# Seven instead of five Strassen pairs in the second feed-forward product, with two sums of weight blocks added by DMA

## The chip, the core and the metric

The kernel runs on one core of a Trainium2 chip. The metric is the device time of one execution in microseconds, the median over runs. A profile is one execution with every instruction, semaphore event and DMA recorded. TensorE is called PE here, VectorE DVE, ScalarE ACT, GpSimd POOL, SyncE SP.

## The reference

One layer of a decoder trunk over 256 positions of width 1024: RMS norm, attention with 8 heads of 128 (one block of 256, causal), residual add, RMS norm, a SwiGLU mixer with 2816 hidden columns, residual add, final RMS norm. All in float32. What the change touches is the last product of the SwiGLU:

```python
def swiglu(h, w_in, w_out):
    g, u = jnp.split(jnp.einsum('bsd,df->bsf', h, w_in), 2, axis=-1)
    return jnp.einsum('bsf,fd->bsd', jax.nn.silu(g) * u, w_out)
```

Here `silu(g) * u` is 256 x 2816 and `w_out` is 2816 x 1024.

## The kernel before

Every float32 product is made of three matmuls of a faster kind (`mm`, L93): an operand is split into a high half (a cast on ACT) and a low half (a subtraction on DVE), and high x high, high x low and low x high are added in PSUM. So every weight tile of 128 x 2048 that a DMA brings (`raw`) has to be turned into `hi` and `lo` before PE can use it. The pool `wpool` has four buffers of each of these three; `weights()` takes the next one of each, and a buffer comes free when its last reader has finished.

The second product adds up over NC = 11 row-tile pairs of `w_out` (256 rows each, laid out as 128 x 2048). A plain pair takes `eight_mm`: 8 products of 128 x 128 by 128 x 512, 24 matmuls. A pair whose number is in SEVEN (L49) takes `seven_mm` (L426): Strassen's scheme for the 2 x 2 blocks, 7 products, 21 matmuls. It needs four sums of blocks of the hidden activations, made once in `turn` (L361), and four sums of weight blocks, made in `load_out` (L390): the first two by one add of 1024 columns on DVE (L404), then one each of 512 columns (L410, L412). A Strassen pair therefore takes two buffers of `raw`, `hi` and `lo`: the first for the plain blocks, of which 1536 columns are split, the second (`rs`, `hs`, `ls`) for the four sums.

The order of the pairs is 0 to 8 (`TAIL` = 9), then pairs 9 and 10, which are always plain and are split over the output corners at the end, so that the final norm can begin early. The seven PSUM accumulators of Strassen's scheme live through all pairs; the plain pairs add into four of them (`corners`), and after pair 8 the corner sums are put together on DVE (L457 to L466). `turn` of a pair runs on PE, ACT and DVE beside the first product (`hidden`), one pair behind it. Which instruction of DVE, ACT and SP stands before which is fixed when the program is built; each engine works its list in order, and an instruction that waits holds up all behind it. All loads of weights go through SP's queue; POOL has nothing to do after the start.

`held` (L65) lets big tiles that are used one after another share memory; `HAT` gives the columns that a pair takes in them, 896 for a Strassen pair, 512 for a plain one.

Of the kernel before, what the change touches and what calls it, by code (L numbers as in the profile page):

```python
# [26 lines left out]
F32 = mybir.dt.float32  # L27
F32R = mybir.dt.float32r
AF = mybir.ActivationFunctionType
ALU = mybir.AluOpType  # L30
AX = mybir.AxisListType

P = 128
T = 256
# [3 lines left out]
H = 8  # L38
# [7 lines left out]
XK = 4  # L46


SEVEN = (0, 2, 4, 6, 8)  # L49
HALF = 5  # L50
HAT = [sum(896 if d in SEVEN else 512 for d in range(c)) for c in range(NC + 1)]


@with_exitstack
def trunk(ctx, tc, xT, x, g2, g3, wv, wqk, wo, w_in, w_out, out):
    nc = tc.nc
# [8 lines left out]
    def held(n, dtype, slot):  # L65
        return home.tile([P, SLOTS[slot]], dtype, name=slot)[:, :n]
# [7 lines left out]
    def weights():  # L74
        return [wpool.tile([P, 2048], d, name=n) for d, n in ((F32, "raw"), (F32R, "hi"), (F32R, "lo"))]
# [12 lines left out]
    def load(src, pieces=2):  # L88
        tiles = weights()
        fetch(tiles, src, 0, 2048, pieces)  # L90
        return tiles[1:]

    def mm(o, lh, ll, rh, rl, first, last):  # L93
        nc.tensor.matmul(o, lhsT=lh, rhs=rh, start=first, stop=False)  # L94
        nc.tensor.matmul(o, lhsT=lh, rhs=rl, start=False, stop=False)  # L95
        nc.tensor.matmul(o, lhsT=ll, rhs=rh, start=False, stop=last)  # L96
# [39 lines left out]
    with tc.tile_pool(name="attn2", bufs=2) as a2:  # L136
        xh = const.tile([P, KD, T], F32R, name="xh")
        xl = const.tile([P, KD, T], F32R, name="xl")
        oh, ol = held(2 * H * T, F32R, "first").rearrange("p (i h t) -> i p h t", i=2, h=H)

        third = held(D + T + 18 * P, F32, "third")
        v1, rbc = third[:, :D], third[:, D : D + T]
# [4 lines left out]
        for k in range(KD):  # L147
# [13 lines left out]
            else:  # L161
                a = k % 2 * 1024
# [40 lines left out]
        def project(h):  # L203
            wh, wl = (w.rearrange("p (k n) -> p k n", k=KD) for w in wk.pop(h))
            pk = ps_a.tile([P, 2, T], F32, name="pa") if h < 2 else ps_mm.tile([P, 2, T], F32, name="pmm")
            for j in range(2):
                js = slice(j * P, (j + 1) * P)
                for k in range(KD):
                    mm(pk[:, j], wh[:, k, js], wl[:, k, js], xh[:, k], xl[:, k], k == 0, k == KD - 1)

            f = a2.tile([P, 2 * T], F32, name="qk")
            nc.vector.tensor_tensor(
                f.rearrange("p (j t) -> p j t", j=2), pk, rbc[:, None, :].to_broadcast([P, 2, T]), op=ALU.mult
            )
            fh = a2.tile([P, 3 * P], F32R, name="qkh")
            fl = a2.tile([P, 3 * P], F32R, name="qkl")
            nc.scalar.copy(fh, f[:, P:])
            nc.vector.tensor_sub(fl, f[:, P:], fh.bitcast(F32))
            qk[h] = f, fh, fl
# [22 lines left out]
        def transpose_p(h):  # L242
            pp = ps_a.tile([P, 3 * P], F32, name="pa")
            for i in range(3):
                nc.tensor.transpose(pp[:, i * P : (i + 1) * P], pn[h][:, i * P : (i + 1) * P], ident)  # L245
            p0h = a2.tile([P, T], F32R, name="p0h")
            p0l = a2.tile([P, T], F32R, name="p0l")
            p1 = a2.tile([P, P], F32, name="p1")
            nc.scalar.copy(p0h, pp[:, :T])
            nc.vector.tensor_sub(p0l, pp[:, :T], p0h.bitcast(F32))  # L250
            nc.scalar.copy(p1, pp[:, T:])
            pt[h] = p0h, p0l, p1
# [11 lines left out]
        def follow(h):  # L264

            for step, i in ((attend, h - 3), (scores, h - 1), (transpose_p, h - 2)):
                if 0 <= i < H:
                    step(i)

        for h in range(H):  # L270
            if h > 1:
                wk[h] = load(wqk[h])
            project(h)
            follow(h)
# [48 lines left out]
    with tc.tile_pool(name="ffn2", bufs=2) as f2:  # L323
# [3 lines left out]
        def parts(a, b):  # L327

            at = HAT[HALF]
            return hh[:, a:b], (hls[0][:, a:b] if a < at else hls[1][:, a - at : b - at])  # L330
# [23 lines left out]
        def split(at, src):  # L354

            to = parts(at, at + int(np.prod(src.shape[1:])))
            h, l = (t.rearrange("p (a b) -> p a b", a=src.shape[1]) for t in to)
            nc.scalar.copy(h, src)
            nc.vector.tensor_sub(l, src, h.bitcast(F32))

        def turn(c, ph=None):  # L361
            if ph is None:
                ph = ps_a.tile([P, 2, T], F32, name="pa")
            for j in range(2):
                for t in range(NT):
                    nc.tensor.transpose(ph[:, j, t * P : (t + 1) * P], hs_[c, t][:, j * P : (j + 1) * P], ident)  # L366
            if c not in SEVEN:
                split(HAT[c], ph)
                return
            a11, a21, a12, a22 = (ph[:, j, t * P : (t + 1) * P] for j in range(2) for t in range(NT))  # L370
            split(HAT[c], ph[:, 0:1, :P])
            split(HAT[c] + P, ph[:, 1:2])
            fs = f2.tile([P, 4, P], F32, name="fs")
            fc = f2.tile([P, 2, P], F32, name="fc")
            nc.scalar.copy(fc, ph[:, :, P:])

            nc.vector.tensor_sub(fs[:, 0], a21, fc[:, 1])
            nc.vector.tensor_add(fs[:, 1], a11, fc[:, 0])
            nc.vector.scalar_tensor_tensor(fs[:, 2], fs[:, 0], -1.0, a11, op0=ALU.mult, op1=ALU.subtract)
            nc.vector.tensor_add(fs[:, 3], a12, fs[:, 2])  # L380
            split(HAT[c] + 3 * P, fs)
# [8 lines left out]
        def load_out(c):  # L390
            if c not in SEVEN:
                return load(w_out[c])

            raw, hi, lo = tiles = weights()
            rs, hs, ls = weights()
            nc.sync.dma_start(raw, w_out[c])

            def part(r, h, l, a, b):
                nc.scalar.copy(h[:, a:b], r[:, a:b])  # L399
                nc.vector.tensor_sub(l[:, a:b], r[:, a:b], h[:, a:b].bitcast(F32))  # L400

            part(raw, hi, lo, 0, 1536)

            nc.vector.tensor_tensor(  # L404
                rs[:, :1024].rearrange("p (a b) -> p a b", a=2),
                raw[:, 512:1536].rearrange("p (a b) -> p a b", a=2),
                raw[:, None, 1536:].to_broadcast([P, 2, 512]),
                op=ALU.add,
            )
            nc.vector.tensor_add(rs[:, 1024:1536], rs[:, :512], raw[:, 1024:1536])  # L410
            part(rs, hs, ls, 0, 1024)
            nc.vector.tensor_add(rs[:, 1536:], rs[:, 1024:1536], raw[:, :512])  # L412
            part(rs, hs, ls, 1024, 2048)
            return hi, lo, hs, ls

        def bank(pool, n=512):
            return pool.tile([P, n], F32, name="pmm" if pool is ps_mm else "pb" if pool is ps_b else "pa")
# [5 lines left out]
        SIDES = {2: (1, 0, 0), 1: (0, 0, 1), 3: (6, 0, 2), 7: (4, 2, 1), 5: (3, 2, 0), 6: (5, 2, 2), 4: (2, 2, 3)}  # L423
        begun = set()

        def seven_mm(c, ws):  # L426
            for i, (a, w, b) in SIDES.items():
                e = slice(b * 512, (b + 1) * 512)
                mm(acc7[i], *parts(HAT[c] + a * P, HAT[c] + (a + 1) * P), ws[w][:, e], ws[w + 1][:, e], i not in begun, c == SEVEN[-1] and i in (1, 5, 6, 7))
                begun.add(i)  # L430

        def eight_mm(c, ws, t, a, n, o, first=False, last=False):
            for j in range(2):
                at = HAT[c] + j * T + t * P
                e = slice(j * D + a, j * D + a + n)
                mm(o, *parts(at, at + P), ws[0][:, e], ws[1][:, e], first and j == 0, last and j == 1)

        TAIL = NC - 2
        wu = {}
        for c in range(TAIL):  # L440
            wu[c] = load_out(c)
            if c in SEVEN:
                seven_mm(c, wu[c])
                if c == 0:
                    turn(NC - 1, ph_last)
                    corners = {(0, 0): acc7[2], (0, 512): acc7[3], (1, 0): acc7[4], (1, 512): bank(ps_a)}
            else:
                for (t, a), o in corners.items():
                    eight_mm(c, wu[c], t, a, 512, o, (t, a) == (1, 512) and c == 1)
        for c in range(TAIL, NC):  # L450
            wu[c] = load_out(c)

# [26 lines left out]
        for i, (t, o, (a, b), (ra, rb)) in enumerate(plan):  # L479
            for c in range(TAIL, NC):  # L480
                eight_mm(c, wu[c], t, a, b - a, o[:, : b - a], o is last and c == TAIL, c == NC - 1)

# [27 lines left out]
def _layouts(x, attn_norm, attn_w_qkv, attn_w_o, ffn_norm, ffn_w_in, ffn_w_out, final_norm):  # L510
# [5 lines left out]
    def rows(a):  # L516

        n = a.shape[0] // (2 * P)
        return a.reshape(n, 2, P, D).transpose(0, 2, 1, 3).reshape(n, P, 2 * D)
# [3 lines left out]
    w_out = rows(ffn_w_out[0])  # L523
    for c in SEVEN:

# [33 lines left out]
```

## Time and profile before

| | us |
|---|---|
| median of 3 runs | 299.97 (299.95 to 300.65) |
| the profiled execution | 299.56 |
| its span, first to last instruction | 297.8 |
| PE busy | 290.2 |
| DVE busy | 210.9 |
| ACT busy | 167.9 |

Matmuls overlap: the profile gives each 0.39 us while they begin every 0.23 us, so the pace is read from start to start. A row of the timeline gives the start in us from the span's beginning, the length, the engine and the line; "x3" are instructions merged into one row. A row of the waits says who waited, for whom, for how long in total, how often, and the longest.

### The profile page before, as it was taken

To read this page: it belongs to the slowest core of one execution; us is meant where nothing else is said; L and a number is where in the kernel's file an instruction comes from. 1 tells how busy PE (TensorE), PEld (TensorE's weight loads), DVE (VectorE), ACT (ScalarE), POOL (GpSimd) and SP (SyncE) were. 2 spreads that over 40 slices of the span, in tenths; PEclk is the share of its full clock that TensorE was granted. 3 is DMA by queue.
4 is the path that set the end of the run, shared out by engine and by line. 5 is a ranking of instruction groups with operands and counts; after the bars stand their busy time and mean duration, and the time that the engine had idled before them with its cause. 6 is when DMAs were issued, how large, how long until landed. Compare 5 with 4: busy or idle time off the path is not lost.

```text
span 297.8 us, 4015 instructions
## 1 busy us (share of the span) xinstructions
PE 290.2 (97%) x1544; PEld 247.6 (83%) x1544; DVE 210.9 (71%) x328; ACT 167.9 (56%) x272; POOL 1.3 (0%) x8
## 2 busy tenths in 40 slices
PE   7999999999999999999999999999999999999992
PEld 4788999999988888888888888888888888888881
DVE  4756988777776587657647647749857698888684
ACT  4786886555555496555455446446426647445443
POOL 1000000000000000000000000000000000000000
PEclk9999999999999999999999999999999999999998
DMA  6999895644445406764365465352333444670003
GB/s 200 383 411 418 289 351 194 236 146 151 142 156 190 165 36 222 281 261 155 141 241 183 143 227 196 141 196 88 141 144 119 163 158 145 262 252 31 2 0 141
DMA packets 10099, 55.84 MB, mean 188 GB/s; under 512 B 1120, under 2 KB 2656, under 8 KB 4192
## 3 DMA queue, kind: packets, MB, share of 16 engines
q1 hardware_dynamic: 9648, 55.06, 50.7%
q10 hardware_dynamic: 432, 0.52, 0.5%
q8 instruction: 12, 0.20, 0.3%
q14 instruction: 7, 0.06, 0.1%
HBM read 54.53 MB, written 1.05 MB: 187 GB/s over the span
## 4 chain that ended last, share of the span: by engine, by line
PE 94%; DMA 2%; DVE 1%; ACT 1%; SPq 1%; issue 0%
PE pmm L96 23%; PE pmm L94 23%; PE pmm L95 23%; PE pmm L179 7%; PE pb L96 2%; PE pb L94 2%; PE pb L95 2%; PE pa L94 2%; PE pa L96 2%; PE pa L95 2%; DMA raw<-in_wv 2%; PE pa L366 2%; PE pa L245 1%; PE pb L224 1%; PE pb L260 1%; PE pb L300 1%
## 5 line engine op out<-in xcount | busy, mean ns | idle before, releaser
L86 DVE TENSOR_TENSOR lo<-raw,hi 128x1024 fp32r<-128x1024 f32 (+2 forms) x91 | 106.4, 1185 | 38.9 <-ACT hi L85 38.6
L85 ACT CAST hi<-raw 128x1024 fp32r<-128x1024 f32 (+2 forms) x91 | 90.8, 1021 | 50.1 <-PE pmm L96 23.7
L94 PE MATMUL pmm<-hi,xh 128*128 128x512 f32 x176 | 69.6, 396 | 0.0
L96 PE MATMUL pmm<-hi,xl 128*128 128x512 f32 x176 | 68.7, 390 | 0.0
L95 PE MATMUL pmm<-lo,xh 128*128 128x512 f32 x176 | 68.5, 389 | 0.0
L96 PEld LDWEIGHTS pmm<-hi,xl 128*128 128x128 f32 x176 | 33.0, 188 | 7.1
L95 PEld LDWEIGHTS pmm<-lo,xh 128*128 128x128 f32 x176 | 33.1, 188 | 6.6
L94 PEld LDWEIGHTS pmm<-hi,xh 128*128 128x128 f32 x176 | 33.0, 188 | 6.5
L94 PE MATMUL pmm<-hi,first 128*128 128x512 f32 x76 | 30.3, 398 | 0.0
L95 PE MATMUL pmm<-lo,first 128*128 128x512 f32 x76 | 29.6, 389 | 0.0
L94 PE MATMUL pmm<-xh,hi 128*128 128x256 f32 x96 | 27.6, 287 | 0.0
L96 PE MATMUL pmm<-xh,lo 128*128 128x256 f32 x96 | 27.1, 283 | 0.0
L95 PE MATMUL pmm<-xl,hi 128*128 128x256 f32 x96 | 27.1, 283 | 0.0
L348 ACT ACTIVATE sg<-pmm,r 128x256 f32<-128x256 f32 x22 | 10.4, 475 | 28.8 <-PE pmm L96 28.6
L399 ACT CAST hi<-raw 128x1024 fp32r<-128x1024 f32 (+1 forms) x15 | 17.5, 1193 | 14.9 <-issue 6.6
L400 DVE TENSOR_TENSOR lo<-raw,hi 128x1024 fp32r<-128x1024 f32 (+1 forms) x15 | 20.4, 1398 | 6.2 <-ACT hi L399 6.1
L350 DVE SCALAR_TENSOR_TENSOR hs<-pmm,r,sg 128x256 f32<-128x256 f32 x22 | 10.6, 483 | 14.9 <-ACT sg L348 14.9
L95 PEld LDWEIGHTS pmm<-xl,hi 128*128 128x128 f32 x96 | 18.4, 192 | 0.0
L96 PEld LDWEIGHTS pmm<-xh,lo 128*128 128x128 f32 x96 | 18.4, 191 | 0.0
L94 PEld LDWEIGHTS pmm<-xh,hi 128*128 128x128 f32 x96 | 18.4, 191 | 0.0
L95 PEld LDWEIGHTS pmm<-lo,first 128*128 128x128 f32 x76 | 14.3, 188 | 2.8
L94 PEld LDWEIGHTS pmm<-hi,first 128*128 128x128 f32 x76 | 14.3, 188 | 2.7
(143 smaller groups left out, 425.5 us busy)
## 6 DMA issues: line engine op xcount, KB each, us to landing
raw<-in_w_in SPq DMA_DIRECT2D x22, 1024.0 KB, 4.8
raw<-in_w_out SPq DMA_DIRECT2D x11, 1024.0 KB, 4.8
raw<-in_wqk SPq DMA_DIRECT2D x8, 1024.0 KB, 7.4
raw<-in_wo SPq DMA_DIRECT2D x4, 1024.0 KB, 4.8
raw<-in_wv SPq DMA_DIRECT2D x7, 512.0 KB, 7.7
second<-in_xT SPq DMA_DIRECT2D x8, 128.5 KB, 6.8
x_sb<-in_x SPq DMA_DIRECT2D x1, 1024.0 KB, 9.5
g_bc<-in_g SPq DMA_DIRECT2D x2, 512.0 KB, 5.5
```

The costliest lines, as they stand in the source:

```text
L85: nc.scalar.copy(hi[:, s], raw[:, s])
L86: nc.vector.tensor_sub(lo[:, s], raw[:, s], hi[:, s].bitcast(F32))
L94: nc.tensor.matmul(o, lhsT=lh, rhs=rh, start=first, stop=False)
L95: nc.tensor.matmul(o, lhsT=lh, rhs=rl, start=False, stop=False)
L96: nc.tensor.matmul(o, lhsT=ll, rhs=rh, start=False, stop=last)
L179: nc.tensor.matmul(pv[t][a // 512][:, a % 512 : a % 512 + b - a], lhsT=l[:, k, t * P : (t + 1) * P], rhs=r[:, a:b],  start=k == 0 and a % ...
L224: nc.tensor.matmul(ps[:, :P], lhsT=f[:, :P], rhs=f[:, T : T + P], start=True, stop=True)
L348: nc.scalar.activation(sg, pf[t][:, 0], AF.Silu, scale=r2[t])
L350: nc.vector.scalar_tensor_tensor(hs_[c, t], pf[t][:, 1], r2[t], sg, op0=ALU.mult, op1=ALU.mult)
L366: nc.tensor.transpose(ph[:, j, t * P : (t + 1) * P], hs_[c, t][:, j * P : (j + 1) * P], ident)
L399: nc.scalar.copy(h[:, a:b], r[:, a:b])
L400: nc.vector.tensor_sub(l[:, a:b], r[:, a:b], h[:, a:b].bitcast(F32))
```

## The change

SEVEN becomes (0, 1, 3, 4, 5, 7, 8): of the pairs before the last two, only 2 and 6 stay plain. In `load_out` the first load brings 1536 instead of 2048 columns. The add of 1024 columns on DVE is gone: columns 512 to 1535 are loaded a second time, into the second buffer, and a DMA from POOL's queue adds columns 1536 to 2047 to both halves of it (`accum_op`). In the last Strassen pair the products come in the order 1, 6, 5, 7, 2, 3, 4 instead of 2, 1, 3, 7, 5, 6, 4. The memory that two more Strassen pairs need comes from the attention stage's small tiles, which move into `first`, and from single buffers for `fs` and `fc`.

```diff
-SEVEN = (0, 2, 4, 6, 8)
+SEVEN = (0, 1, 3, 4, 5, 7, 8)
...
-        oh, ol = held(2 * H * T, F32R, "first").rearrange("p (i h t) -> i p h t", i=2, h=H)
+
+        first = held(2 * H * T + 20 * P, F32R, "first")
+        oh, ol = first[:, : 2 * H * T].rearrange("p (i h t) -> i p h t", i=2, h=H)
+        head_qk = first[:, 2 * H * T : 2 * H * T + 12 * P].rearrange("p (b i n) -> b i p n", b=2, i=2)
+        head_p0 = first[:, 2 * H * T + 12 * P :].rearrange("p (b i n) -> b i p n", b=2, i=2)
...
-            fs = f2.tile([P, 4, P], F32, name="fs")
-            fc = f2.tile([P, 2, P], F32, name="fc")
+            fs = f2.tile([P, 4, P], F32, name="fs", bufs=1)
+            fc = f2.tile([P, 2, P], F32, name="fc", bufs=1)
...
-            nc.sync.dma_start(raw, w_out[c])
+            nc.sync.dma_start(raw[:, :1536], w_out[c][:, :1536])
...
+            nc.sync.dma_start(rs[:, :1024], w_out[c][:, 512:1536])
+            nc.gpsimd.dma_start(
+                rs[:, :1024].rearrange("p (a b) -> p a b", a=2),
+                w_out[c][:, None, 1536:].to_broadcast([P, 2, 512]),
+                accum_op=ALU.add,
+            )
             part(raw, hi, lo, 0, 1536)
-
-            nc.vector.tensor_tensor(
-                rs[:, :1024].rearrange("p (a b) -> p a b", a=2),
-                raw[:, 512:1536].rearrange("p (a b) -> p a b", a=2),
-                raw[:, None, 1536:].to_broadcast([P, 2, 512]),
-                op=ALU.add,
-            )
...
-            for i, (a, w, b) in SIDES.items():
+            for i in (1, 6, 5, 7, 2, 3, 4) if c == SEVEN[-1] else SIDES:
+                a, w, b = SIDES[i]
...
+        PLAIN = [c for c in range(TAIL) if c not in SEVEN]
...
-                    eight_mm(c, wu[c], t, a, 512, o, (t, a) == (1, 512) and c == 1)
+                    eight_mm(c, wu[c], t, a, 512, o, (t, a) == (1, 512) and c == PLAIN[0])
```

What stands in the engines' lists now. First DVE, from the sums of pair 6 to the low halves of pair 8 before the change; `lo<-raw,hi` is a low half, `raw<-raw` a sum of weight blocks:

```order
L404 TENSOR_TENSOR raw<-raw 128x1024
L410 TENSOR_TENSOR raw<-raw 128x512
L412 TENSOR_TENSOR raw<-raw 128x512
L400 TENSOR_TENSOR lo<-raw,hi 128x1536
L400 TENSOR_TENSOR lo<-raw,hi 128x1024 x2
L86 TENSOR_TENSOR lo<-raw,hi 128x1024 x2
L404 TENSOR_TENSOR raw<-raw 128x1024
L410 TENSOR_TENSOR raw<-raw 128x512
L412 TENSOR_TENSOR raw<-raw 128x512
L400 TENSOR_TENSOR lo<-raw,hi 128x1536
L400 TENSOR_TENSOR lo<-raw,hi 128x1024 x2
```

A pair's sums stand ahead of its own low halves, and nothing of another pair stands between. And now, on the same engine, from the sums of pair 5 (L412, L414) through the low halves of the plain pair 6 (L86) to those of pairs 7 and 8 (L402):

```order
L412 TENSOR_TENSOR raw<-raw 128x512
L414 TENSOR_TENSOR raw<-raw 128x512
L402 TENSOR_TENSOR lo<-raw,hi 128x1024
L86 TENSOR_TENSOR lo<-raw,hi 128x1024
L402 TENSOR_TENSOR lo<-raw,hi 128x1024
L86 TENSOR_TENSOR lo<-raw,hi 128x1024
L402 TENSOR_TENSOR lo<-raw,hi 128x1536
L412 TENSOR_TENSOR raw<-raw 128x512
L414 TENSOR_TENSOR raw<-raw 128x512
L402 TENSOR_TENSOR lo<-raw,hi 128x1024
L402 TENSOR_TENSOR lo<-raw,hi 128x1536
L402 TENSOR_TENSOR lo<-raw,hi 128x1024
```

The low halves of neighbouring pairs are now mixed, and the low half of the 1536 plain columns of a pair comes ahead of that pair's sums.

Second, POOL's list, where the seven accumulating DMAs of pairs 0, 1, 3, 4, 5, 7 and 8 stand behind the work of the start; the names in brackets are the semaphores that each waits for, `DMAHW` those of loads, `DMASW` those of accumulations:

```order
L406 DMA raw<-in_w_out 128x2x512 [waits DMAHW4_49,DMAHW3_49,DMAHW6_49,DMAHW2_49,DMAHW7_49,DMAHW0_49,DVE_49]
L406 DMA raw<-in_w_out 128x2x512 [waits DMAHW2_49,DMAHW5_49,DMAHW1_49,DMAHW6_49,DVE_49,Activation_49]
L406 DMA raw<-in_w_out 128x2x512 [waits DMAHW5_49,DMAHW1_49,DVE_49]
L406 DMA raw<-in_w_out 128x2x512 [waits DMAHW7_49,DMAHW3_49,DVE_49]
L406 DMA raw<-in_w_out 128x2x512 [waits DMAHW1_49,DMASW2_49,DVE_49]
L406 DMA raw<-in_w_out 128x2x512 [waits DMAHW0_49,DMASW0_49,DMAHW4_49,DVE_49,Activation_49]
L406 DMA raw<-in_w_out 128x2x512 [waits DMAHW2_49,DMAHW6_49,DMASW1_49,DVE_49]
```

Before, POOL issued no DMA; now each waits for the load of the same columns, which itself waits for a free buffer.

Third, PE in pair 8, its first four products; `hi_2489` and `lo_2490` hold the plain blocks, `hi_2492` the sums, and the tile at the left is the accumulator. Before:

```order
L94 MATMUL pb_2198<-hi_2489,first_1248 128x512
L95 MATMUL pb_2198<-lo_2490,first_1248 128x512
L96 MATMUL pb_2198<-hi_2489,third_1250 128x512
L94 MATMUL pb_2199<-hi_2489,first_1248 128x512
L95 MATMUL pb_2199<-lo_2490,first_1248 128x512
L96 MATMUL pb_2199<-hi_2489,third_1250 128x512
L94 MATMUL pmm_2200<-hi_2489,first_1248 128x512
L95 MATMUL pmm_2200<-lo_2490,first_1248 128x512
L96 MATMUL pmm_2200<-hi_2489,third_1250 128x512
L94 MATMUL pmm_2201<-hi_2492,first_1248 128x512
L95 MATMUL pmm_2201<-lo_2493,first_1248 128x512
L96 MATMUL pmm_2201<-hi_2492,third_1250 128x512
```

Now `hi_2495` holds the plain blocks and `hi_2498` the sums:

```order
L94 MATMUL pb_2189<-hi_2495,first_1216 128x512
L95 MATMUL pb_2189<-lo_2496,first_1216 128x512
L96 MATMUL pb_2189<-hi_2495,third_1218 128x512
L94 MATMUL pmm_2193<-hi_2498,first_1216 128x512
L95 MATMUL pmm_2193<-lo_2499,first_1216 128x512
L96 MATMUL pmm_2193<-hi_2498,third_1218 128x512
L94 MATMUL pa_2192<-hi_2498,first_1216 128x512
L95 MATMUL pa_2192<-lo_2499,first_1216 128x512
L96 MATMUL pa_2192<-hi_2498,third_1218 128x512
L94 MATMUL pmm_2191<-hi_2498,first_1216 128x512
L95 MATMUL pmm_2191<-lo_2499,first_1216 128x512
L96 MATMUL pmm_2191<-hi_2498,third_1218 128x512
```

The sums of this pair are read from its second product on, where they were read from its fourth.

## Rows read from the trace of the kernel before

**Rows 1.** The page's busy times: us, share of the span, instructions.
```profile
PE 290.2 (97%) x1544; PEld 247.6 (83%) x1544; DVE 210.9 (71%) x328; ACT 167.9 (56%) x272; POOL 1.3 (0%) x8
```
**Rows 2.** Timeline of PE: start of the second product, of pair 8, and behind it.
```profile
234.62 0.48 PE L94 MATMUL pb<-hi,first 128*128 128x512 f32 x1
...
276.04 0.39 PE L94 MATMUL pb<-hi,first 128*128 128x512 f32 x1
...
280.80 0.39 PE L94 MATMUL pb<-hi,first 128*128 128x512 f32 x1
```
**Rows 3.** Busy time by stretch of the span, columns in the first line.
```profile
core 0: us, PE busy (x) PEld busy (x) DVE busy (x) ACT busy (x) POOL busy (x), PEclk, DMA share, GB/s
120.00:150.00 30.00, 30.00 (x138) 24.81 (x137) 18.79 (x25) 15.06 (x22) 0.00 (x0) 1.00 0.56 203
...
245.00:270.00 25.00, 25.00 (x112) 20.71 (x111) 21.63 (x21) 14.33 (x13) 0.00 (x0) 1.00 0.57 213
...
270.00:284.00 14.00, 14.00 (x64) 11.58 (x63) 9.97 (x12) 5.31 (x7) 0.00 (x0) 1.00 0.01 1
```
**Rows 4.** Timeline of DVE and ACT: one `turn`, then low halves of pairs 5, 6, 8.
```profile
227.46 0.37 ACT L375 COPY fc<-pa 128x256 f32<-128x256 f32 x1 [1.09 <-DVE third L359]
...
228.07 0.28 DVE L378 TENSOR_TENSOR fs<-pa,fc 128x128 f32<-128x128 f32 x1
...
229.97 0.61 ACT L358 CAST first<-fs 128x512 fp32r<-128x512 f32 x1
...
231.24 0.69 DVE L359 TENSOR_TENSOR third<-fs,first 128x512 fp32r<-128x512 f32 x1
...
251.53 2.36 DVE L86 TENSOR_TENSOR lo<-raw,hi 128x1024 fp32r<-128x1024 f32 x2 [0.34 <-ACT hi L85]
...
257.40 4.03 DVE L400 TENSOR_TENSOR lo<-raw,hi 128x1536 fp32r<-128x1536 f32 x3 [0.92 <-ACT hi L399]
...
267.60 4.03 DVE L400 TENSOR_TENSOR lo<-raw,hi 128x1536 fp32r<-128x1536 f32 x3 [0.64 <-ACT hi L399]
```
**Rows 5.** Waits of SP's queue in 195 to 280: us in total, times, longest.
```profile
SPq L81 <- DVE lo L400: 21.6, 3, 7.6
SPq L396 <- DVE lo L86: 20.9, 5, 6.1
```
**Rows 6.** Instructions on `raw` from 200 on: ns min/median/max, first and last start.
```profile
L86 DVE TENSOR_TENSOR lo<-raw,hi x18: 1212/1220/1226, 201.8 to 278.5; 128x1024 fp32r<-128x1024 f32 x18
...
L400 DVE TENSOR_TENSOR lo<-raw,hi x15: 1215/1219/1759, 219.2 to 270.4; 128x1024 fp32r<-128x1024 f32 x10, 128x1536 fp32r<-128x1536 f32 x5
...
L404 DVE TENSOR_TENSOR raw<-raw x5: 1216/1217/1226, 204.6 to 264.3; 128x1024 f32<-128x1024 f32 x5
...
L412 DVE TENSOR_TENSOR raw<-raw x5: 682/691/693, 210.2 to 266.3; 128x512 f32<-128x512 f32 x5
...
DMA to landing us min/median/max: 4.7/4.8/4.9
```
**Rows 7.** DMA queues (packets, MB, share), and issues with median us from issue to landing.
```profile
q1 hardware_dynamic: 9648, 55.06, 50.7%
q10 hardware_dynamic: 432, 0.52, 0.5%
q8 instruction: 12, 0.20, 0.3%
q14 instruction: 7, 0.06, 0.1%
...
raw<-in_wqk SPq DMA_DIRECT2D x8, 1024.0 KB, 7.4
...
g_bc<-in_g SPq DMA_DIRECT2D x2, 512.0 KB, 5.5
out_y<-xh SPq DMA_DIRECT2D x2, 320.0 KB, 2.5
```
**Rows 8.** Timeline of SP's queue: the fourth and the seventh buffer taken for `w_out`.
```profile
216.20 0.33 SPq L396 DMA_DIRECT2D raw<-in_w_out  x1
...
233.09 0.33 SPq L396 DMA_DIRECT2D raw<-in_w_out  x1
```

More of the change, by code (lines that the diff above doesn't have):

```diff
@@ L214, in project @@
             )
-            fh = a2.tile([P, 3 * P], F32R, name="qkh")
-            fl = a2.tile([P, 3 * P], F32R, name="qkl")
+            fh, fl = head_qk[h % 2]
             nc.scalar.copy(fh, f[:, P:])
@@ L245, in transpose_p @@
                 nc.tensor.transpose(pp[:, i * P : (i + 1) * P], pn[h][:, i * P : (i + 1) * P], ident)
-            p0h = a2.tile([P, T], F32R, name="p0h")
-            p0l = a2.tile([P, T], F32R, name="p0l")
+            p0h, p0l = head_p0[h % 2]
             p1 = a2.tile([P, P], F32, name="p1")
```

## The prediction

> **What bounds the kernel now.** I read the page first: TensorE (PE) is busy 97% of the span, VectorE (DVE) 71%, ScalarE (ACT) 56%, GpSimd (POOL) 1.3 us in all [rows 1]. Then the second product, the stage that the change touches. It starts on PE at 234.62 us [rows 2] and its last matmul runs near 290. In 245 to 284 PE has no idle time, at full granted clock, and DVE is busy in 21.63 of 25 us, then 9.97 of 14 [rows 3]. So PE bounds this stage, with DVE close behind. PE's step is read from the starts of pair 8 and of what follows it: 280.80 - 276.04 is 21 matmuls of 512 columns, 0.227 us each [rows 2]; that is one Strassen pair (7 products x 3), 4.77 us; a plain pair has 24, 5.45 us.
>
> The other thing to see is the lead of the preparation. The last low half of pair 8 ends at 267.60 + 4.03 = 271.63 [rows 4], and PE begins that pair at 276.04 [rows 2]: 4.4 us early. For pair 6 the end is 261.43 [rows 4], PE's start 276.04 - 4.77 - 5.45 = 265.82: again 4.4. The lead is constant since the four slots of each weight buffer hold it there, not DVE's pace. SyncE's loads show the same: its waits are for DVE's releases, 21.6 and 20.9 us [rows 5], and a load lands 4.8 us after issue [rows 6].
>
> **What is removed.** Two pairs go from 24 matmuls to 21: 6 x 0.227 = 1.36 us of PE. On DVE a Strassen pair now costs 1.76 + 0.69 + 1.22 + 0.69 + 1.22 = 5.58 us instead of 6.80, the 1.22 us add of L404 being gone [rows 6]. Seven of those and two plain pairs (2 x 1.22 each) are 43.9 us; before it was 5 x 6.80 + 4 x 2.44 = 43.8. So DVE is not relieved overall: what is gained per pair goes to two more pairs.
>
> **What is added in the hidden stage.** Pairs 1, 3, 5, 7 get the four sums in `turn`, 2 and 6 lose them: net two more. Each costs four adds of 128 columns and one split of 512, 4 x 0.28 + 0.69 = 1.8 us of DVE, and 0.37 + 0.61 us of ACT [rows 4], in a loop where DVE is busy 18.79 of 30 us with no idle PE [rows 3]. Hidden; if its cover were gone it would be under 2 us on DVE, not on PE. The single buffer of `fs` is reused one `hidden` (48 matmuls, 10.9 us) later, so it holds nothing back. The head tiles inside `first` keep two sets: nothing.
>
> **What is added on the path of the sums.** Before: one 1 MB load, then an add on DVE. Now: a load of 1536 columns, a second load of 1024 columns into the slot for the sums, and, only when that has landed, an accumulating DMA from POOL into the same tile; only then may DVE and ACT start on the sums. Two latencies in a row stand where there was one. The second load is 0.5 MB: between 320 KB in 2.5 us and 1 MB in 4.8 [rows 6, 7] it comes to 3.1 by the straight line, while the half MB of `g_bc` took 5.5 in the median [rows 7]; I take 3.5. The accumulation, from POOL's issue to landing, I call A. No row shows one: POOL issues no DMA and no software queue appears in rows 7. It reads 0.5 MB from HBM and 0.5 MB of its own destination. Lower bound: the 0.5 MB plain line, 3.1 us (no reason excludes a little less, 2.5, but below 3.6 the time is the same anyway, see below). Upper bound: 7.4, the 1 MB loads of `wqk` that had other loads before them in the queue [rows 7]. A 1 MB load alone, with as many bytes read, takes 4.8. I take **A = 5.5**: above 4.8, because in at least four of the seven cases the next load of 0.75 or 1 MB is in flight on the same engines, and it is the measured median of a half-MB load.
>
> The Trainium skill's page "DMA: Bandwidth & Descriptors" (section "Anatomy of one DMA — SWDGE (gpsimd) path") gives 2.0 us plus bytes over 436 GB/s for a DMA that POOL issues: an estimate of 3.2 us here, and by it the accumulation would be hidden; with both reads counted it would be 4.4. No run here shows either.
>
> **The sum, walked forward.** The order of each engine is fixed, so I go along it with these durations; neighbouring DVE rows overlap by some 0.08 us (two of 1.22 take 2.36 [rows 4]). PE without stalls reaches pair 0 at 234.6, 1 at 239.9, 2 at 244.6, 3 at 250.1, 4 at 254.8, 5 at 259.6, 6 at 264.4, 7 at 269.8, 8 at 274.6; a pair's sums are wanted 9 matmuls (2.04 us) later, in pair 8, which now starts 1, 6, 5, 7, after 3 (0.68).
> The slot of pair 3's sums is the seventh buffer taken, filled at 233.09 before [rows 8]; its load is now issued at 235.5, because pair 1's sums come late: their load goes out near 217.6 (the fourth buffer was filled at 216.20 before [rows 8], one more wait for a release is in between), lands at 221.1, is accumulated at 226.7, and behind the add that waits for it stand some 8 us of DVE work and 0.8 of waits for ACT, the last of it the 1.76 us low half that frees the slot. It lands at 239.1, is accumulated by 244.6. Then DVE does, in order, add 0.69, split 0.68, low half 1536 1.76, low half 1.22, add 0.69, pair 4's low half 1.76, low half 1.22: 7.6 us with overlaps, to 252.3, which frees the slot for pair 5's sums. Load to 255.9, accumulation to 261.4, two adds and a low half to 263.9: PE wants it at 261.6 + 0.23, **2.1 us late**. The second low half stands behind one of pair 6 (to 266.3), PE wants it 1.4 us after the first: 1.0 more. The adds free the next slot at 262.9: load of pair 7 to 266.6, accumulation to 272.1, first low half 274.7, which PE, now 3.2 late, wants at 275.05; the second, behind pair 8's 1536 columns, ends at 277.7, 1.1 late. Pair 8: slot free at 267.5, loaded 271.9, accumulated 277.4, third quarter ready at 281.4 against a PE that wants it near 279.7: 1.7. Stalls: 2.1 + 1.0 + 1.1 + 1.7 = **5.9 us**. The low halves of pairs 9 and 10 push DVE's corner sums back too, some 0.6 us at the end. Sum: 5.9 + 0.6 - 1.4 = **+5.1 us**.
> The same walk at other A, net: 3.6 or less, no loss, -1.4; 3.9, -0.9; 4.4, even; 4.8, +1.7; 7.0, +12.7; 7.4, +14.7. Beyond 4.4 a microsecond of A costs 5, because the sums of pairs 0, 1, 3, 5 and 7 follow each other through slots and DVE's order. The walk is linear arithmetic on rows, so I trust it to about 1 us for a given A.
> The profiled run took 299.56 us for a span of 297.8 (1.8 around it), 0.41 under the median of 299.97. 299.56 + 5.1 = 304.7; against the median **305.1 us**.
>
> **Rivals.**
> (a) The accumulation is quick, A under 3.9 with its neighbours: no wait is new, PE keeps its pace and only the 1.36 us count: 298.6 us. For it: a lead of 4.4 us, and DMA engines at a 0.57 share of this stage [rows 3]. Against: it needs less than a 1 MB load alone (4.8), though it reads as many bytes and shares the queues. Chance 0.25. The Trainium skill's 3.2 us speaks for this rival.
> (b) In between, 3.9 to 4.6: stalls of 0.5 to 2 us eat the gain, 299.1 to 300.9; chance 0.11.
> (c) My forecast, A from 4.6 to 7, 301 to 312.7: chance 0.52.
> (d) Slower still: A over 7, so that the waiting adds, first in DVE's order, also hold the `hs` products and splits of the last hidden pairs and PE stalls already before 245: 313 us and more, from A = 7; chance 0.12. For it: DVE is in order and pairs 0 and 1 are accumulated while the hidden stage runs.
>
> **How the numbers follow.** About 0.3%, 0.9 us, is what a measurement of this kernel can tell from no change. Faster: (a), 0.25. Same: (b), 0.11. Slower: (c) and (d), 0.64. The range reaches down to (a)'s 298.6 with 0.4 for the spread, and up to A = 7: 298.2 to 312.7, leaving out (d) and little else. The likeliest case's own range is 301 to 312.7.
>
> **What would show it.** In the profile after: a software DMA queue with seven issues, whose landing time is A; PE's idle before L95 and L94 reading the sums' `hi` and `lo`, worst in pairs 5, 7 and 8; DVE's L412 and L414 waiting for the DMA; 1538 instead of 1544 matmuls. I am wrong if A is under 3.9, if the second load lands much faster than 3.5, or if PE stalls elsewhere.

## The result, and the profile after

The changed kernel takes **324.45 us** (median of 4 runs, 322.83 to 325.56) against 299.96 (299.8 to 300.65): ratio 1.0807, 95% interval 1.078 to 1.0834, 24.5 us slower. The forecast was 305.1, in a range to 312.7. The profiled execution took 324.39 us for a span of 322.6. Ratios here and below are of the mean times, and of e13 one slow run (326.18 us, granted clock 0.959) is left out.

The page after, to be read beside [rows 1, 7]: busy times, the software queue, the chain of work by engine and by line, two groups of instructions (busy us, mean ns | idle before them and what ended it), and the DMA issues with the median us to landing.

```profile
PE 296.6 (92%) x1538; PEld 249.8 (77%) x1538; DVE 213.3 (66%) x341; ACT 171.6 (53%) x280; POOL 9.8 (3%) x15
...
q0 software_dynamic: 1904, 3.67, 6.9%
...
PE 67%; DMA 12%; DVE 11%; issue 4%; ACT 3%; SPq 1%; POOLq 0%; ACTq 0%
...
L401 ACT CAST hi<-raw 128x1024 fp32r<-128x1024 f32 (+1 forms) x21 | 24.8, 1193 | 33.5 <-DMA raw<-in_w_out 29.8
...
L412 DVE TENSOR_TENSOR raw<-raw 128x512 f32<-128x512 f32 x7 | 4.8, 691 | 33.8 <-DMA raw<-in_w_out 26.9
...
raw<-in_w_out SPq DMA_DIRECT2D x7, 768.0 KB, 4.9
...
raw<-in_w_out SPq DMA_DIRECT2D x7, 512.0 KB, 3.9
raw<-in_w_out POOLq DMA_DIRECT2D x7, 512.0 KB, 8.0
```

The announced six matmuls are gone (1538) and the seven software transfers are there. **A, the adding transfer from POOL's issue to landing, is 8.0 us**, where I took 5.5 and bounded it at 7.4. ACT and DVE wait 29 and 27 us for it (0.6 of ACT's 29.8 are for a plain load), and DMA is 12% of the chain that ended last.

Where PE loses the time: the busy times by stretch, columns as in [rows 3], first three whole stretches, then two short ones.

```profile
230.00:255.00 25.00, 22.11 (x93) 17.28 (x91) 14.01 (x21) 9.88 (x14) 1.19 (x1) 0.93 0.58 145
255.00:280.00 25.00, 16.14 (x61) 11.84 (x62) 16.65 (x17) 10.71 (x11) 2.38 (x2) 0.86 0.66 185
280.00:300.00 20.00, 16.21 (x60) 11.83 (x59) 12.99 (x13) 8.26 (x8) 2.38 (x2) 0.92 0.86 227
...
242.40:245.80 3.40, 3.36 (x10) 2.69 (x10) 3.40 (x5) 3.07 (x4) 0.17 (x1) 0.50 0.47 152
...
273.10:283.30 10.20, 5.53 (x12) 4.07 (x13) 7.31 (x7) 5.26 (x5) 1.20 (x1) 0.50 0.31 93
```

PE, which before had no idle time in 245 to 284 [rows 3], is idle for 2.9, 8.9 and 3.8 us of these stretches, and DVE is not the busy one in its place: 16.65 of 25 us, less than before. No other engine is full in its place; a transfer is under way. The last two lines show a second loss: the granted clock falls to half, 1.2 GHz, at the end of the 2.0 us gap below and within the 6.3 us one, and stays there for 3.4 and 10.2 us.

PE's timeline names what ends the gaps (start us, us, instruction [idle before, releaser]):

```profile
235.68 0.48 PE L94 MATMUL pb<-hi,first 128*128 128x512 f32 x1
...
239.48 0.47 PE L94 MATMUL pa<-hi,first 128*128 128x512 f32 x1 [0.78 <-DVE fs L382]
242.44 0.80 PE L94 MATMUL pmm<-hi,first 128*128 128x512 f32 x1 [2.02 <-DVE hs L352]
255.99 0.51 PE L94 MATMUL pa<-hi,first 128*128 128x512 f32 x1 [1.08 <-DVE third L361]
262.20 0.50 PE L95 MATMUL pmm<-lo,first 128*128 128x512 f32 x1 [0.85 <-DVE lo L402]
...
277.18 0.80 PE L94 MATMUL pmm<-hi,first 128*128 128x512 f32 x1 [6.32 <-ACT hi L401]
...
279.58 0.63 PE L94 MATMUL pa<-hi,first 128*128 128x512 f32 x1
280.01 0.63 PE L95 MATMUL pa<-lo,first 128*128 128x512 f32 x1
```

The first row is the start of the second product. The longest gap, 6.32 us, is the wait for the sums of pair 5. The last two rows are 0.43 us apart where [rows 2] had 0.227: matmuls at half clock.

What stood behind that gap, in the chain that ended last (start us, us, what):

```profile
258.74 0.60 DVE raw L414
259.34 1.15 DVE lo L402
260.49 0.44 issue
260.93 1.23 DVE lo L402
262.15 0.02 issue
262.17 4.37 DMA raw<-in_w_out
...
267.10 8.83 DMA raw<-in_w_out
275.93 0.02 issue
275.96 0.70 DVE raw L412
```

Read it as one loop: a low half on DVE frees the slot (262.15), the second load fills it (4.37), POOL adds into it (8.83), and only then does DVE's L412 run. From the moment at which its slot is free, the pair's sums cost 13.2 us of transfer.

In the hidden stage the same wait does what rival (d) said. DVE's timeline:

```profile
233.93 0.69 DVE L412 TENSOR_TENSOR raw<-raw 128x512 f32<-128x512 f32 x1 [7.56 <-DMA raw<-in_w_out]
234.54 0.48 DVE L352 SCALAR_TENSOR_TENSOR hs<-pmm,r,sg 128x256 f32<-128x256 f32 x1
```

DVE stood 7.56 us before an add of pair 1, with an `hs` product of the hidden stage next in its order. The two rows of PE that had to wait before 245 (0.78 us at 239.48, 2.02 at 242.44) were released by DVE's rows behind that add, which DVE worked without another stall of 0.3 us.

**The account.** The span is 24.8 us longer. From the last matmul to the end there are 6.1 us before (297.8 - 291.71) and 8.0 after (322.6 - 314.56): 1.9 us, since the last corner sums stand behind other late work on DVE. The remaining 22.9 us, with the 1.4 saved added, are 24.2 on PE. Of these, 1.1 us are there when the second product begins (235.68 against 234.62 in [rows 2]); they arise in the first 40 us of this execution, and experiment 1's kernel, with all of the change but the transfers, begins it at 234.77, so they are not shown to belong to the change. Counting starts of its matmuls, 13 steps of over 0.5 us hold some 19 us beyond a normal step. The matmuls at half clock (22 in the two short stretches, at most 0.43 - 0.227 too long each, so under 4.5 us) are 3 to 4, and slightly longer steps make up the rest.

### The profile page after: what moved, and what is told of

It is laid out like the page before. It is cut to its first block, busy times and chain, and to the rows that moved or that the text cites. A ratio compares the mean times of both kernels' runs of the same rounds, so it can differ in the third digit from the quotient of the medians.

```text
span 322.6 us, 4076 instructions
## 1 busy us (share of the span) xinstructions
PE 296.6 (92%) x1538; PEld 249.8 (77%) x1538; DVE 213.3 (66%) x341; ACT 171.6 (53%) x280; POOL 9.8 (3%) x15
## 4 chain that ended last, share of the span: by engine, by line
PE 67%; DMA 12%; DVE 11%; issue 4%; ACT 3%; SPq 1%; POOLq 0%; ACTq 0%
PE pmm L95 17%; PE pmm L96 17%; PE pmm L94 17%; DMA raw<-in_w_out 10%; PE pmm L183 6%; DVE lo L402 5%; DMA raw<-in_wv 2%; ACT hi L401 2%; PE pa L95 1%; PE pa L94 1%; PE pa L96 1%; DVE lo L86 1%; PE pa L368 1%; DVE raw L412 1%; PE pa L248 1%
## 5 line engine op out<-in xcount | busy, mean ns | idle before, releaser
L86 DVE TENSOR_TENSOR lo<-raw,hi 128x1024 fp32r<-128x1024 f32 (+2 forms) x87 | 101.7, 1183 | 34.3 <-ACT hi L85 34.1
L85 ACT CAST hi<-raw 128x1024 fp32r<-128x1024 f32 (+2 forms) x87 | 86.9, 1019 | 42.3 <-PE pmm L96 21.6
L401 ACT CAST hi<-raw 128x1024 fp32r<-128x1024 f32 (+1 forms) x21 | 24.8, 1193 | 33.5 <-DMA raw<-in_w_out 29.8
L94 PE MATMUL pmm<-hi,first 128*128 128x512 f32 x76 | 32.1, 422 | 9.2 <-ACT hi L401 7.2
L95 PE MATMUL pmm<-lo,first 128*128 128x512 f32 x76 | 31.4, 414 | 4.3 <-DVE lo L402 4.3
L402 DVE TENSOR_TENSOR lo<-raw,hi 128x1024 fp32r<-128x1024 f32 (+1 forms) x21 | 29.0, 1396 | 1.2 <-ACT hi L401 1.1
L412 DVE TENSOR_TENSOR raw<-raw 128x512 f32<-128x512 f32 x7 | 4.8, 691 | 33.8 <-DMA raw<-in_w_out 26.9
L350 ACT ACTIVATE sg<-pmm,r 128x256 f32<-128x256 f32 x22 | 10.2, 474 | 22.4 <-PE pmm L96 22.4
L95 PEld LDWEIGHTS pmm<-lo,first 128*128 128x128 f32 x76 | 15.0, 197 | 9.1 <-DVE lo L402 6.3
```

The source lines that it names most:

```text
L85: nc.scalar.copy(hi[:, s], raw[:, s])
L86: nc.vector.tensor_sub(lo[:, s], raw[:, s], hi[:, s].bitcast(F32))
L350: nc.scalar.activation(sg, pf[t][:, 0], AF.Silu, scale=r2[t])
```

## The experiments

**Theory** (T): the whole loss is the chain of two transfers in front of the sums; its length, not the seven pairs or the order, sets the time. **Rivals**: the other parts of the change cost something (order, places of the pairs); or it is only the software queue of POOL that is slow (Q); or only the amount that is added (S). The expectations below, each on record before its run, use letters of their own.

### 1. The sums on DVE again, all else as changed

```
-            nc.sync.dma_start(raw[:, :1536], w_out[c][:, :1536])
+            nc.sync.dma_start(raw, w_out[c])
-            nc.sync.dma_start(rs[:, :1024], w_out[c][:, 512:1536])
-            nc.gpsimd.dma_start(... accum_op=ALU.add)
             part(raw, hi, lo, 0, 1536)
+            nc.vector.tensor_tensor(rs[:, :1024]..., raw[:, 512:1536]..., raw[:, None, 1536:]..., op=ALU.add)
```

> The changed kernel with the two sums of weight blocks made by DVE again, from one load of 2048 columns; seven Strassen pairs and the new order of the last pair stay. Theory L (the loss is the 8.0 us from issue to landing of the accumulating DMA, in a chain of buffers): the loss is gone and the six matmuls count, walked forward no PE stall, 299.0 us (-0.9). Rival B (seven pairs want two buffers each with few plain pairs between, whatever makes the sums): most of the loss stays, over 310. Rival K (the granted clock falls by itself in this stage): it stays at 0.97 and the time above 304.

298.77 us, ratio 0.9968 (0.9957 to 0.998): the other parts gain 1.0 us. Its stretches, columns as in [rows 3]:

```profile
245.00:270.00 25.00, 25.00 (x112) 20.71 (x111) 24.17 (x23) 13.85 (x12) 0.00 (x0) 1.00 0.53 200
270.00:284.00 14.00, 14.00 (x64) 11.58 (x63) 13.96 (x17) 7.01 (x9) 0.00 (x0) 1.00 0.23 85
```

PE is gapless at full clock again. DVE, at 24.17 of 25 and 13.96 of 14 us, has nothing left: this is what the change meant to relieve, and an eighth pair would hardly be hidden (not tried).

### 2. The parts alone: adding with five pairs, and the order

Five pairs as before, with the sums by DMA (label e2); the kernel before with the new order of the last pair alone (label e3):

```
 e2, against after:
-SEVEN = (0, 1, 3, 4, 5, 7, 8)
+SEVEN = (0, 2, 4, 6, 8)
-            for i in (1, 6, 5, 7, 2, 3, 4) if c == SEVEN[-1] else SIDES:
+            for i in SIDES:
 e3, against before:
-            for i, (a, w, b) in SIDES.items():
+            for i in (1, 6, 5, 7, 2, 3, 4) if c == SEVEN[-1] else SIDES:
+                a, w, b = SIDES[i]
```

> The accumulating DMA alone: five Strassen pairs (0, 2, 4, 6, 8) as before, their sums by the second load and the accumulation, old order of the last pair. Theory L: a plain pair stands between any two Strassen pairs, but 3.9 + 8.0 us still stand in each chain; walked forward with 8.0, PE stalls of 10.8 us, net +12.8, and some 2 to 4 us more where the clock is halved behind the longest stalls: 312 to 317. Rival B: no loss, 299 to 301.

> The kernel before with only the order of the last pair's products changed to 1, 6, 5, 7, 2, 3, 4. All theories: PE has no stall and the corner sums are not late, so within 0.3 us of 299.97. If the order itself costs, PE would wait for the sums of pair 8, and the time is over 301.

Adding with five pairs: 318.4 us, ratio 1.0626 (1.0604 to 1.0649), 1.4 us above the range that was expected. The order alone: 299.72, ratio 1.0 (0.9986 to 1.0014). So the transfers cost 18.7 us even without the two more pairs, and the order nothing, as the prediction had it.

### 3. The transfer as a plain copy: by POOL, and by SyncE

```
             nc.gpsimd.dma_start(          (label e5: nc.sync.dma_start)
                 rs[:, :1024]..., w_out[c][:, None, 1536:].to_broadcast([P, 2, 512]),
-                accum_op=ALU.add,
             )
```

> The changed kernel with POOL's DMA copying instead of adding (same shape, same queue, same waits; the sums are not made, the block of columns 1536 to 2047 stands in their place). Theory S (the add is what is slow: packets of 2 KB take 178 ns each where 8 KB of a load take 309, since each reads twice): landing falls to 4.5 to 5.5 us, and by the walk the time is 300 to 306. Rival Q (POOL's queue is what is slow: descriptors made by POOL, 1.2 us, and loads that go first, so that the first packet comes 1.9 to 5.1 us after issue): landing stays over 6.5, the time over 310.

> As the copy from POOL (the sums are not made, the block of columns 1536 to 2047 stands in their place), but the third DMA goes out from SP's queue; the same three steps in a row, load, wait, second DMA into the same tile. Theory Q (POOL's queue, 6.5 us for a copy, is what is slow): a half-MB DMA from SP lands in 3.5 to 4 us, the chain fits under the lead, 299 to 301 us. Rival C (the chain of two DMAs in one buffer is too long whatever the queue): over 305.

POOL's copy: 317.56 us, ratio 1.0588 (1.0561 to 1.0615). SyncE's: 316.32, ratio 1.0561 (1.0535 to 1.0587). One line of each, POOL's copy first: the landing of the transfer at L406, us min/median/max.

```profile
DMA to landing us min/median/max: 5.4/6.5/7.3
```

```profile
DMA to landing us min/median/max: 5.6/5.9/8.6
```

Both of my cheap explanations fell. Adding is worth 1.5 us of the 8.0 against a plain copy of the same shape, and a hardware queue instead of the software queue another 0.6. In the second of these the next pair's loads also stand in SyncE's queue behind a wait for the second load, so the two are not a clean pair; but the queue alone is not the cause.

### 4. Half of what is added

```
             nc.gpsimd.dma_start(
-                rs[:, :1024].rearrange("p (a b) -> p a b", a=2),
-                w_out[c][:, None, 1536:].to_broadcast([P, 2, 512]),
+                rs[:, :512],
+                w_out[c][:, 1536:],
                 accum_op=ALU.add,
```

> The changed kernel with the accumulating DMA adding to the first half alone (0.25 MB, 128 x 512; the second of the two sums is left unadded). Theory Q: most of the 8.0 us is queue and start, so landing stays at 6 to 7 us, and the walk with 6.5 gives stalls of 12 us, with the clock 313 to 317. Theory S (bytes): landing halves to 4 to 5 us, 300 to 305 us.

315.5 us, ratio 1.0522 (1.0507 to 1.0537). The landing at L406:

```profile
DMA to landing us min/median/max: 4.1/6.1/7.6
```

Half of the bytes saves 1.9 of the 8.0 us. S alone falls: if the other half is worth as much, 3.8 us of A go with the amount and 4.2 do not.

### 5. The sums on POOL's own adder, and another place for the seven pairs

```
 e7, against e1:
-            nc.vector.tensor_tensor(rs[:, :1024]..., op=ALU.add)
+            nc.gpsimd.tensor_tensor(rs[:, :1024]..., op=ALU.add)
 e8, against e1:
-SEVEN = (0, 1, 3, 4, 5, 7, 8)
+SEVEN = (0, 1, 2, 4, 5, 7, 8)
```

> Seven pairs, one load of 2048 columns, the two sums made by POOL's own add of 1024 columns instead of DVE's or the DMA's. No row shows such an add. If it takes up to 3 us, the walk has no stall and DVE is relieved by 1.22 us per pair: 298.4 to 298.8. At 4 us it is 303, at 6 us over 315. If POOL's reads hold DVE's subtractions up, DVE's 1.22 us rows get longer while it runs.

> Seven pairs with the two sums on DVE as in the first experiment, plain pairs 3 and 6 instead of 2 and 6. The walk has no stall and the corner sums are 0.4 us less late than with 2 and 6: 298.4 against 298.8 measured there. If the place of the plain pairs does not matter, 298.8.

On POOL: 303.8 us, ratio 1.0127 (1.0114 to 1.014), a miss. The instructions on `raw` (ns min/median/max, first and last start):

```profile
L402 DVE TENSOR_TENSOR lo<-raw,hi x21: 1212/1219/3967, 220.1 to 278.4; 128x1024 fp32r<-128x1024 f32 x14, 128x1536 fp32r<-128x1536 f32 x7
...
L406 POOL TENSOR_TENSOR raw<-raw x7: 2399/2613/3993, 205.2 to 267.3; 128x1024 f32<-128x1024 f32 x7
...
L412 DVE TENSOR_TENSOR raw<-raw x7: 676/694/2877, 207.7 to 273.2; 128x512 f32<-128x512 f32 x7
```

POOL's add takes 2.6 us, and rows of DVE stretch beside it: the low half of 1536 columns that starts at 267.53 to 3.97 us (1.76 was the longest before, [rows 6]), the add of 0.69 that starts at 249.68 to 2.88. Where DVE's low halves were the first to run, they kept their 1.22 us and POOL's adds beside them took 3.99 and 3.51. The Trainium skill's page "SBUF — State Buffer" (section "Who interferes with whom") says that a DVE instruction with two SBUF inputs contends with a GpSimd instruction that reads SBUF; these rows agree.

The other place of the pairs: 298.52 us (298.15 to 300.07), ratio 0.9961 (0.9948 to 0.9974), the fastest of all that were run and faster than both kernels. Against the first experiment it is 0.25 us, inside the intervals: whether the place matters is not settled.

### 6. What makes the transfer long: shape, chain, or adding

Three edits of the second step: whole rows from SyncE as the second step (e9); no second step at all, POOL's queue alone loads the tile (e11); adding, but from whole rows (e13).

```
 e9, in place of the adding transfer:
+            nc.sync.dma_start(rs[:, :1024], w_out[c][:, 512:1536])
 e11, in place of both transfers into rs:
+            nc.gpsimd.dma_start(rs[:, :1024], w_out[c][:, 512:1536])
 e13, in place of the adding transfer:
+            nc.gpsimd.dma_start(rs[:, :1024], w_out[c][:, 512:1536], accum_op=ALU.add)
```

> The adding transfer is replaced by a repeat of the second load: SyncE's queue loads the same 512 KB of columns 512 to 1535 once more into the same tile, in whole rows of 4 KB instead of one 2 KB block read twice (so the sums are not made). The copy of the broadcast block from the same queue took 5.8 to 6.1 us and the kernel 316.3 us. Theory shape: the 5.8 us came from the rows of 2 KB read twice; whole rows land as the second load itself did, in 3.9 to 4.3 us, and by the slope of the runs so far (6.1 us gave 315.5, 8.0 us gave 324.5: 4.7 us for each us of the second step) the time is 303 to 308 us. Theory chain: any second transfer into a buffer that has to wait for the first meets the next pair's loads on the way and lands in 5.5 us or more; the time stays at 314 to 317 us.

> There is no second load by SyncE and no addition: GpSimd's software queue alone loads columns 512 to 1535 into the tile of the sums (so the sums are not made), with nothing to wait for but the buffer. Theory chain: what costs is that one transfer stands behind another; alone, GpSimd's load lands at 5 to 6.5 us after its issue, beside the 768 KB load, where the two in a row took 3.9 + 8.0 = 11.9 us; preparation finds its data and the time is 298.5 to 300.5 us. Theory software queue: the queue as such is late (6.5 us and more for each transfer, more beside loads); landing 7 us or more and 302 to 308 us, with VectorE and ScalarE waiting for it in the pairs 5, 7 and 8.

> The adding transfer reads whole rows of 4 KB (columns 512 to 1535, added to themselves, so the sums are other sums) instead of one 2 KB block read twice; the bytes that are written stay 512 KB. Theory addition: the adding write sets the 8.0 us, and the shape of what is read does nothing; landing 7.5 to 8.5 us and 322 to 327 us. Theory shape: the 2 KB block read twice makes the transfer long; landing 6.5 us or less and 314 to 319 us.

Times: e9 306.24 us, ratio 1.0214 (1.0155 to 1.0273); e11 298.62, ratio 0.9957 (0.9942 to 0.9971); e13 323.25, ratio 1.0739 (1.0673 to 1.0805). The landing of that transfer (L406, in e11 L405), min/median/max, in this order:

```profile
DMA to landing us min/median/max: 3.6/4.2/6.6
```

```profile
DMA to landing us min/median/max: 3.9/4.0/4.7
```

```profile
DMA to landing us min/median/max: 5.4/7.6/9.0
```

And the software queue of e11, then of e13 (packets, MB, share of 16 engines):

```profile
q0 software_dynamic: 1008, 3.67, 3.8%
```

```profile
q0 software_dynamic: 1008, 3.67, 6.5%
```

Each run says one thing. e11: **the software queue is not slow**; one transfer with nothing in front of it lands in 4.0 us and the time is that of the sums on DVE. e13: **the shape does little to the addition**; reading whole rows makes 7.6 of 8.0. The queue's share gives the packets: 3.8% of 16 engines over a span of 296.3 us, for 1008 packets, is 0.18 us each; 6.5% of 321.5 is 0.33. The same bytes, in packets of the same size, hold the DMA engines almost twice as long when they are added. e9: for the plain copy by SyncE the shape counts, 5.9 against 4.2 us and 316.3 against 306.2 (both with SyncE's later loads held up behind the second step); but even a second step as quick as the first leaves the kernel 6.2 us behind.

### 7. The same chain, started earlier

```
+            nc.sync.dma_start(rs[:, :1024], w_out[c][:, 512:1536])
             nc.sync.dma_start(raw[:, :1536], w_out[c][:, :1536])
-            nc.sync.dma_start(rs[:, :1024], w_out[c][:, 512:1536])
```

> The changed kernel with the two loads of SyncE in the other order: the 512 KB that are added to come first, the 768 KB behind them; all else as in the changed kernel. Theory chain: what sets the stalls is the end of the two transfers in a row, and it comes earlier by what the first one gains, about 0.7 us of issue and up to 1 us of shared bandwidth; at 4.7 us for each us of it the time is 316 to 321 us. Rival: the addition is then issued in the middle of the 768 KB load and becomes as much longer as the load becomes shorter; the time stays within 322.5 to 326 us, with an addition over 8.3 us.

311.76 us, ratio 1.0392 (1.0361 to 1.0423): 12.7 us faster than the changed kernel by exchanging two lines, more than either theory gave. SyncE's timeline of the changed kernel, then of this one, where L398 is the load that is issued first:

```profile
200.03 0.33 SPq L398 DMA_DIRECT2D raw<-in_w_out  x1
205.89 0.33 SPq L405 DMA_DIRECT2D raw<-in_w_out  x1
210.81 0.33 SPq L398 DMA_DIRECT2D raw<-in_w_out  x1
222.86 0.33 SPq L405 DMA_DIRECT2D raw<-in_w_out  x1
```

```profile
199.57 0.33 SPq L398 DMA_DIRECT2D raw<-in_w_out  x1
205.43 0.33 SPq L399 DMA_DIRECT2D raw<-in_w_out  x1
210.35 0.33 SPq L398 DMA_DIRECT2D raw<-in_w_out  x1
218.00 0.33 SPq L399 DMA_DIRECT2D raw<-in_w_out  x1
```

Rows 1 and 2 of each are pair 0, rows 3 and 4 pair 1. The first slot of pair 0 is free 5.9 us before the second, and whichever load is issued first gets it: the two calls of `weights()` stand in the same order in both kernels. Pair 1's slots are 12.1 us apart in the changed kernel, those of the later pairs 1.1 to 11.4. There the 768 KB, for which the low half of the plain columns waits, get the early slot, while the chain of two begins at 205.89 and 222.86. Here it begins at 199.57 and 210.35, and the plain load in the late slot lands from 7 us before the chain's end to 2 us after it. The addition still takes 7.3 us in the median. I had counted on 0.7 us of issue and 1 of bandwidth and had not seen that the slots move.

## Why the prediction was right or wrong

**The sign and the place were right.** PE waits for the sums of pairs 5, 7 and 8, DVE's L412 waits for the DMA, 1538 matmuls, nothing from the order, nothing from the two more `turn`s in the hidden stage: as predicted, and experiment 1 shows that what is left without the transfers is a gain of 1.0 us (walk: 1.4 without loss). But the last sign of being wrong, "if PE stalls elsewhere", came true as well: 2.8 us before 245, and 1.08 and 0.85 us at 255.99 and 262.20.

**The step that failed is "I take A = 5.5".** A is 8.0, beyond even the 7.4 that I gave as the upper bound. No row of before showed an adding transfer, and I took the durations of plain transfers of as many bytes as both its ends (one point of the lower line, 320 KB in 2.5 us, is even a store). Experiment 6 shows one thing that was missing: the same bytes hold the engines 0.33 instead of 0.18 us per packet. The trace after shows another. Of its seven additions, three have no load of SyncE issued within 2 us of them (227.51, 255.81, 288.46) and land in 6.4, 6.5 and 6.8 us; four have one within 1.1 us (210.19, 245.63, 267.10, 281.51) and land in 8.0 to 8.9. The chain that ended last holds one of each: pair 5's at 267.10, shown above with 8.83 us, and pair 1's:

```profile
227.51 6.39 DMA raw<-in_w_out
```

So 5.5 was too short even for an addition without such a neighbour, and the allowance for neighbours was too small besides; that the neighbour causes the difference was not tested apart. The Trainium skill's page "DMA: Bandwidth & Descriptors" (section "Anatomy of one DMA — SWDGE (gpsimd) path"), whose formula gave an estimate of 3.2 us, comes nearest to the plain transfer alone (4.0 in e11); for the addition behind a load the measurement decides, 8.0.

**The chance of (d) was too small.** With A at 8.0 it is (d) that came true: the waiting adds hold the `hs` products. I gave it 0.12 and left it out of the range.

**The walk: the slope held, the level did not.** The four kernels with a POOL transfer behind the load, against the walk at their A (values between those given are interpolated, 8.0 goes on at 5 us for each):

| kernel | A, us | walk | measured against before |
|---|---|---|---|
| half added (e6) | 6.1 | +8.1 | +15.6 |
| copy (e4) | 6.5 | +10.2 | +17.8 |
| added, whole rows (e13) | 7.6 | +15.7 | +23.2 |
| changed kernel | 8.0 | +17.7 | +24.5 |

From 6.1 to 8.0 the measured slope is 4.7 us for each us of A; the walk said 5. But every row lies about 7 us higher. Four terms of the sum were too small or missing. The second load took 3.9 and not 3.5, which by the slope is 2.0 us. The tail is 1.9 us longer, where I had 0.6. And the halved clock, 3 to 4 us, was not in the sum at all: I walked on at 0.227 us for each matmul behind stalls that I had myself put there. Together these three are 6 to 7 us. The fourth is the walk's first wait:

```profile
218.31 0.69 DVE L412 TENSOR_TENSOR raw<-raw 128x512 f32<-128x512 f32 x1 [5.22 <-DMA raw<-in_w_out]
```

DVE stood 5.22 us before an add of pair 0, and behind that add stands the low half (221.58 to 222.80) that frees the slot for pair 1's second load. That load went out at 222.86, where the walk had "near 217.6" and no wait for pair 0's addition. At pair 1 and pair 4, on the other hand, the additions took 6.4 and 6.5 us and not 8.0. So the terms partly offset each other and their sum proves nothing; they were read from the trace, not tested apart. Even with the right A the walk would have said 317.7.

**The second load** "much faster than 3.5" did not come. That the slot order decides by 1.1 to 12.1 us when the chain begins (experiment 7) was in my walk only as waits for slots; I never asked which of the two loads should have the early one.

**Open.** In the trace's packet records the first packet of the addition leaves 1.9 us after POOL's issue when no load is issued beside it, and 4.0 to 5.1 us after it when SyncE issues one within 0.7 us (245.63 and 245.67; 281.51 and 281.94). Five of the seven transfers of one kernel show it; what delays them was not tried.

## What to carry to other kernels

Work that a DMA took off a busy engine was not free here, since its transfer stood in a row with another one: count the chain from the moment the slot is free to the last landing, and give the longer chain the earlier slot. Where the trace has no row for a kind of transfer, the rows of another kind are not its bound; a kernel that shows that one row is worth more than any interpolation. And where a sum contains stalls of some us on PE, put the slower clock behind them into the sum too.

## What the runs showed of the hardware

- An adding transfer of 512 KB behind a load lands in 8.0 us in the median: 6.4 to 6.8 with no load issued within 2 us of it, 8.0 to 8.9 with one within 1.1 us. Copied instead of added it takes 6.5; half of it added 6.1; as a plain load of whole rows with nothing in front 4.0. Packets of whole rows hold the DMA engines 0.33 us each when added (e13) and 0.18 when loaded (e11).
- The granted clock fell to half for 3.4 us at the end of a 2.0 us stall of PE, and for 10.2 us within and behind one of 6.3 us; matmuls of 512 columns then started 0.43 instead of 0.227 us apart.
- POOL's add of 128x1024 takes 2.4 to 4.0 us where DVE's took 1.22 [rows 6], and two of DVE's rows beside it were stretched, 0.69 to 2.88 us and 1.76 to 3.97.
